# Differential attention in a decoder trunk: weights times values in full fp32 instead of two fp32r halves

## The chip, the core and the metric

The kernel runs as one program on one core of a Trainium2 chip. The metric is the device time of one execution in microseconds; the time quoted for a kernel is the median of its timed runs. One further execution is recorded by the hardware profiler, and all durations of single instructions come from that one.

## The reference

Two layers work on a sequence of 1024 rows of width 1024, everything in float32. Each layer has a token mixer (a convolution group, four heads of differential attention, a gated spatial group, joined by one output projection) and a feed-forward mixer (up-projection, a convolution of width 3, a gate, down-projection). Each ends in a layer norm. The change concerns the attention, which for each head and each block of 128 query rows computes this:

```python
s = jnp.einsum("bhmqd,bhmkd->bhmqk", qb, kb) * scale      # two score maps, m = 0, 1
p = jax.nn.softmax(jnp.where(mask, s, -jnp.inf), axis=-1)
a = p[:, :, 0] - lam * p[:, :, 1]
outs.append(jnp.einsum("bhqk,bhke->bhqe", a, vb))         # vb: 128 values a row
...
o = rms_norm(o, subln_g) * (1.0 - lam_init)
```

## The kernel before

All tensors sit on 128 partitions. Most matrix products are made in the reduced format fp32r: each operand is split into a high part, `hi`, and the rest, `lo`, and three products (hi by hi, hi by lo, lo by hi) are added up in PSUM (`mm3`, L128). A split is a copy by ScalarE and a subtraction by VectorE or GpSimd (`split`, L123).

A layer runs through these stages. `stage1` (L632) makes the projections: first the convolution group's, then the values (`stage_v`, L486), the spatial group (`stage_c`) and queries and keys of four heads (`qk_head`), which go to DRAM. The 62 taps of the depthwise convolution (`conv_taps`, L404) are VectorE work that is handed out in small portions beside these products (`pump`, L93). Then comes the attention (`attention`, L832): four heads, each with eight query blocks of 128 rows, called units here. Unit i reads i+1 key tiles of 128 rows, so a head has 36 key tiles and the two layers together have 288. `stage3` (L909) drives the units, and beside them come the loads of the residual, the splitting of the output projection's weights and the products of the groups that are ready (`out_fill`, L870; tiles `of`). After the attention follow the rest of the output projection (`out_group`, tiles `og`), the norm and the feed-forward mixer.

A unit (`attn_unit`, L742) runs through these steps. TensorE makes two score maps in PSUM (L738, L740). VectorE takes their row maxima (L759, L761). ScalarE makes the exponentials and their row sums (L764). VectorE takes the reciprocals of the sums (L767), a factor `rho` of one number per row (L769), and the difference of the two maps, in place in `p` (L772). TensorE transposes that difference, tile by tile, into PSUM (L783). ScalarE copies it out as the high part (L786) and VectorE makes the low part (L787). TensorE multiplies both with the values (L791, L792). The values `vp` hold a high and a low part side by side, so each product has 256 columns, and the result in PSUM has two halves that still have to be added. ScalarE scales one half (L794), VectorE adds the scaled other half (L795), and ScalarE squares the sum for the norm of the head (L797).

The values get their two parts in `stage_v`: VectorE adds the bias (L492), ScalarE copies the high part (L496), VectorE subtracts (L497), and both go to DRAM in `d_v`.

The order of instructions on each engine is set by a list scheduler at build time, which follows the order of the code, priorities and its own estimates; the up-projection alone has its order written by hand. Buffers come from pools by name: `raw` has 3 buffers, `tmp`, `Ra` and `Rb` have 4 each. `pump` and the late modulation steps are held back until a marked instruction has been issued; for the late steps of layer 0 that mark is `unit_end`, the instruction at L795.

Of the kernel before, what the change touches and what calls it, by code (L numbers as in the profile page):

```python
# [12 lines left out]
F32 = mybir.dt.float32  # L13
F32R = mybir.dt.float32r
BF16 = mybir.dt.bfloat16
I32 = mybir.dt.int32
AF = mybir.ActivationFunctionType
ALU = mybir.AluOpType
AX = mybir.AxisListType

P = 128
D = 1024
S = 1024
L = 2
# [26 lines left out]
class Trunk:  # L51
# [104 lines left out]
    def setup(self):  # L156
        nc, a = self.nc, self.a
        self.ident = self.cst("ident", [P, P])
        make_identity(nc, self.ident)
        self.identb = self.cst("identb", [P, P], BF16)  # L160
        nc.vector.tensor_copy(self.identb, self.ident)
        self.maskb = self.cst("maskb", [P, P], BF16)
        nc.gpsimd.memset(self.maskb, 0.0)
        nc.gpsimd.affine_select(out=self.maskb, in_=self.maskb, pattern=[[-1, P]], compare_op=ALU.is_ge, fill=NEG,
                                base=0, channel_multiplier=1)
        self.ones = self.cst("ones", [P, 1])
        nc.vector.memset(self.ones, 1.0)
        self.mhalf = self.cst("mhalf", [P, 16])
        nc.vector.memset(self.mhalf, -0.5)
        self.cact = self.cst("cact", [P, KT])  # L170
        craw = self.sm("craw", [P, KT], bufs=1)
        nc.sync.dma_start(craw, a["c_t"])
        nc.scalar.activation(out=self.cact, in_=craw, func=AF.Silu)
        self.pc = []
        for l in range(L):
            t = self.cst(f"pc{l}", [P, NPC])
            nc.sync.dma_start(t, a["pcol"][l])
            self.pc.append(t)
        self.rope_c = self.cst("rope_c", [P, 2])
        nc.sync.dma_start(self.rope_c, a["rope_c"])  # L180
        self.lam_cols()
        d = lambda nm, sh, dt=F32: self.dram.tile(list(sh), dt, name=nm, tag=nm, bufs=1)
        self.d_trig = d("d_trig", [2, P, S])
        self.d_q = [d(f"d_q{l}", [4, P, 2, S]) for l in range(L)]
        self.d_k = [d(f"d_k{l}", [4, P, 2, S]) for l in range(L)]
        self.d_v = [d(f"d_v{l}", [4, P, NT, 256]) for l in range(L)]
        self.d_yb = [d(f"d_yb{l}", [2, P, S]) for l in range(L)]
        self.d_xb = d("d_xb", [NT, P, D])
        self.d_act = [d(f"d_act{l}", [NF, P, S]) for l in range(L)]
        self.d_r = [d(f"d_r{l}", [NT, P, D]) for l in range(L)]  # L190
        self.d_gab = d("d_gab", [L, 2, 2 * KT, P])
# [294 lines left out]
    def stage_v(self, l, H, O):  # L486
        nc = self.nc
        brow = self.bias_row(l, 0, 512)

        def evac(tp, ps):  # L490
            vf = self.page("tmp", "vf", shape=(P, 2, 4, P))
            nc.vector.tensor_tensor(out=vf.rearrange("p t h e -> p t (h e)"), in0=ps.rearrange("p (t e) -> p t e", t=2),  # L492
                                    in1=brow.unsqueeze(1).to_broadcast([P, 2, 512]), op=ALU.add)
            for tt in range(2):
                vh = self.page("Ra", "vhl", F32R, (P, 4, 2, P))
                nc.scalar.copy(vh[:, :, 0, :], vf[:, tt])  # L496
                nc.vector.tensor_tensor(out=vh[:, :, 1, :], in0=vf[:, tt], in1=vh[:, :, 0, :].bitcast(F32),  # L497
                                        op=ALU.subtract)
                nc.sync.dma_start(self.d_v[l][:, :, tp * 2 + tt, :].rearrange("h p e -> p h e"),
                                  vh.bitcast(F32).rearrange("p h x e -> p h (x e)"))  # L500
            self.pump(14)
        self.proj_tm(l, 0, H, O, evac)

# [128 lines left out]
    def stage1(self, l, H, O, pre):  # L632
# [31 lines left out]
        for _ in gn:  # L664
            pass
        self.lhs_a(O)
        vp = [self.load_vp(l, 0, i) for i in range(2)]
        self.lhsB, self.lhs0, self.wB = [], [], []
        self.at = O + "c"
        att = self.attention(l, self.X, O, stk, vp, grow)  # L670
# [49 lines left out]
        nc.sync.dma_start(k.bitcast(F32), self.d_k[l][h])  # L720
        return [q[:, 0], q[:, 1], k[:, 0], k[:, 1]]

    def load_vp(self, l, h, i):
        v = self.page("raw", "vp", F32R, (P, 4, 256))
        self.nc.sync.dma_start(v.bitcast(F32), self.d_v[l][h, :, i * 4:(i + 1) * 4, :])
        return v

    def score(self, ps, stk, i):
# [13 lines left out]
    def attn_unit(self, l, at, stk, vp, i, ot, ss):  # L742
# [20 lines left out]
        for m in range(2):  # L763
# [2 lines left out]
        rc = self.sm("rc", [P, 2], bufs=4)  # L766
        nc.vector.reciprocal(out=rc, in_=sums)  # L767
        rho = self.sm("rho", [P, 1], bufs=4)
        nc.vector.scalar_tensor_tensor(out=rho, in0=sums[:, 0:1], scalar=self.nlam[l], in1=rc[:, 1:2],  # L769
                                       op0=ALU.mult, op1=ALU.mult)  # L770
        ad = pr[0]
        nc.vector.scalar_tensor_tensor(out=ad[:, :w], in0=pr[1][:, :w], scalar=rho, in1=ad[:, :w],  # L772
                                       op0=ALU.mult, op1=ALU.add)
        if small:
            a2 = self.page(at, "at", F32R)
            ah, al = a2[:, 0:512], a2[:, 512:1024]
        else:
            ah, al = self.page(at, "ath", F32R), self.page(at, "atl", F32R)
        for b0 in range(0, i + 1, 4):
            b1 = min(i + 1, b0 + 4)  # L780
            pb = self.bank("at")
            for j in range(b0, b1):
                nc.tensor.transpose(pb[:, (j - b0) * P:(j - b0 + 1) * P], ad[:, j * P:(j + 1) * P], self.ident)  # L783
            n = (b1 - b0) * P
            bs = slice(b0 * P, b1 * P)
            nc.scalar.copy(ah[:, bs], pb[:, :n])  # L786
            nc.vector.tensor_tensor(out=al[:, bs], in0=pb[:, :n], in1=ah[:, bs].bitcast(F32), op=ALU.subtract)  # L787
        po = self.bank("pv")
        for j in range(i + 1):
            js = slice(j * P, (j + 1) * P)  # L790
            nc.tensor.matmul(po[:, 0:256], ah[:, js], vp[j // 4][:, j % 4, :], start=j == 0, stop=False)  # L791
            nc.tensor.matmul(po[:, 0:256], al[:, js], vp[j // 4][:, j % 4, :], start=False, stop=j == i)  # L792
        o = ot[:, i, :]
        nc.scalar.activation(out=o, in_=po[:, 128:256], func=AF.Identity, scale=rc[:, 0:1])  # L794
        self.unit_end = nc.vector.scalar_tensor_tensor(out=o, in0=po[:, 0:128], scalar=rc[:, 0:1], in1=o, op0=ALU.mult,  # L795
                                                       op1=ALU.add)
        nc.scalar.activation(out=po[:, 256:384], in_=o, func=AF.Square, accum_out=ss[:, i:i + 1])  # L797

    def head_end(self, l, h, O, ot, ss, halves=(0, 1)):
# [32 lines left out]
    def attention(self, l, H, O, stk, vp, grow):  # L832
        pend = None
        for h in range(4):
            ot = self.page("rows", "ot", shape=(P, NT, P))
            ss = self.sm("oss", [P, NT])
            for n, i in enumerate((7, 6, 3, 5, 2, 4, 1, 0) if h < 3 else (7, 6, 5, 4, 0, 1, 2, 3)):
# [10 lines left out]
                        next(late, None)  # L848
                if n == (1 if h else 4) and h + 1 < 4:
                    nxt = self.load_stacks(l, h + 1, H)  # L850
                    nvp = [self.load_vp(l, h + 1, 0)]
                k = {(2, 3): 0, (2, 5): 1, (2, 7): 2, (3, 0): 3}.get((h, n))
                if k is not None:
                    if k < 2:
                        self.lhs0.append(self.load_yb(l, k, O))
                    self.wB.append(self.load_wout(l, 2 + k, O, grow, self.page(O + "a", "wout")))
                if n == 6 and h + 1 < 4:
                    nvp.append(self.load_vp(l, h + 1, 1))
                if h == 3 and n == 4:
                    self.head_end(l, h, O, ot, ss, (1,))  # L860
                yield
# [571 lines left out]
```

## Time and profile before

| what | value |
|---|---|
| median of 3 runs | 2542.33 us (2537.85 to 2546.43) |
| profiled execution: time, span of its instructions | 2538.86 us, 2537.2 us |
| TensorE busy in the span | 2354.1 us (93%) |
| VectorE busy | 2066.2 us (81%) |
| ScalarE busy | 1066.0 us (42%) |
| GpSimd busy | 395.1 us (16%) |
| mean granted TensorE clock | 0.959 |
| attention stages, by the tiles that TensorE writes | about 290 to 530 us and 1548 to 1795 us |

PE is TensorE's matrix product, PEld its weight load, DVE is VectorE, ACT is ScalarE, POOL is GpSimd, SP issues the DMAs. The recorded end of a product is modelled and products overlap, so TensorE's pace is read from the distance between starts. PEclk is the share of its full clock that TensorE was granted. In a table by stretches, "x96" is the number of instructions that began in the stretch.

### The profile page before, as it was taken

To read this page: it belongs to the slowest core of one execution; us is meant where nothing else is said; L and a number is where in the kernel's file an instruction comes from. 1 tells how busy PE (TensorE), PEld (TensorE's weight loads), DVE (VectorE), ACT (ScalarE), POOL (GpSimd) and SP (SyncE) were. 2 spreads that over 40 slices of the span, in tenths; PEclk is the share of its full clock that TensorE was granted. 3 is DMA by queue.
4 is the path that set the end of the run, shared out by engine and by line. 5 is a ranking of instruction groups with operands and counts; after the bars stand their busy time and mean duration, and the time that the engine had idled before them with its cause. 6 is when DMAs were issued, how large, how long until landed. Compare 5 with 4: busy or idle time off the path is not lost. (4 is left out here: it accounts for less than half of the span.)

```text
span 2537.2 us, 28532 instructions
## 1 busy us (share of the span) xinstructions
PE 2354.1 (93%) x10846; PEld 1912.6 (75%) x10846; DVE 2066.2 (81%) x2794; ACT 1066.0 (42%) x1708; POOL 395.1 (16%) x213
## 2 busy tenths in 40 slices
PE   8999989988999999999789999999899999989996
PEld 7777768766888887788578776777678888868885
DVE  7998787889887888778979987768887777797768
ACT  4314744645554554311131157445554554552111
POOL 1243160433000000000020542213510000000003
PEclk9998979999999999999889998999899999999998
DMA  8443433222332334645513244220322222254311
GB/s 295 152 153 130 160 142 117 75 100 71 112 110 90 117 108 155 206 142 182 172 61 133 87 160 164 95 108 32 108 75 83 84 83 83 84 183 148 100 42 67
DMA packets 88826, 302.47 MB, mean 119 GB/s; under 512 B 9392, under 2 KB 18928, under 8 KB 87152
## 3 DMA queue, kind: packets, MB, share of 16 engines
q1 hardware_dynamic: 88688, 300.65, 34.9%
q8 instruction: 85, 1.39, 0.2%
q14 instruction: 53, 0.43, 0.1%
HBM read 232.42 MB, written 68.19 MB: 118 GB/s over the span
## 5 line engine op out<-in xcount | busy, mean ns | idle before, releaser
L130 PE MATMUL og<-dn,dn 128*128 128x512 f32 x704 | 281.2, 399 | 37.6 <-DVE r L905 21.6
L1092 PE MATMUL upb<-comb,uw 128*128 128x512 f32 x704 | 275.9, 392 | 10.9 <-DVE upc L1116 6.7
L131 PE MATMUL og<-dn,dn 128*128 128x512 f32 x704 | 278.5, 396 | 0.0
L132 PE MATMUL og<-dn,dn 128*128 128x512 f32 x704 | 278.3, 395 | 0.0
L1093 PE MATMUL upb<-comb,uw 128*128 128x512 f32 x704 | 275.4, 391 | 2.7 <-DVE comb L980 2.7
L1094 PE MATMUL upb<-comb,uw 128*128 128x512 f32 x704 | 274.9, 391 | 0.0
L1116 DVE TENSOR_TENSOR uw<-wu,uw 128x512 fp32r<-128x512 f32 x210 | 144.2, 687 | 125.3 <-ACT uw L1119 125.3
L138 POOL TENSOR_TENSOR lnrs<-lnrs,mhalf 128x1 f32<-128x1 f32 x32 | 20.8, 653 | 1386.1 <-DVE lnrs L137 1374.4
L905 DVE TENSOR_TENSOR r<-og,r 128x1024 f32<-128x1024 f32 x144 | 174.6, 1219 | 66.8 <-PE og L132 66.0
L1129 DVE SCALAR_TENSOR_TENSOR cv<-upc,pc,cv 128x1023 f32<-128x1023 f32 (+1 forms) x176 | 225.4, 1281 | 2.8
L130 PEld LDWEIGHTS og<-dn,dn 128*128 128x128 f32 x704 | 134.5, 191 | 72.1 <-DVE r L905 27.2
L410 DVE SCALAR_TENSOR_TENSOR convacc<-convy,pc,convacc 128x1023 f32<-128x1023 f32 (+14 forms) x120 | 178.7, 1489 | 1.8
L125 ACT CAST dn<-actr 128x1024 fp32r<-128x1024 f32 x44 | 46.0, 1049 | 306.5 <-PE og L131 146.2
L1092 PEld LDWEIGHTS upb<-comb,uw 128*128 128x128 f32 x704 | 132.7, 188 | 41.6 <-DVE upc L1116 8.4
L1119 ACT CAST uw<-wu 128x512 fp32r<-128x512 f32 x210 | 121.7, 616 | 83.6 <-DVE wu L1116 77.1
L1093 PEld LDWEIGHTS upb<-comb,uw 128*128 128x128 f32 x704 | 132.8, 189 | 31.8 <-DVE comb L980 4.5
L132 PEld LDWEIGHTS og<-dn,dn 128*128 128x128 f32 x704 | 134.4, 191 | 28.2
L131 PEld LDWEIGHTS og<-dn,dn 128*128 128x128 f32 x704 | 134.8, 192 | 27.4
L1094 PEld LDWEIGHTS upb<-comb,uw 128*128 128x128 f32 x704 | 132.7, 189 | 27.6
L1093 PE MATMUL upd<-comb,uw 128*128 128x512 f32 x352 | 138.1, 392 | 5.9 <-DVE comb L980 5.9
L1092 PE MATMUL upd<-comb,uw 128*128 128x512 f32 x352 | 137.7, 391 | 0.0
L1094 PE MATMUL upd<-comb,uw 128*128 128x512 f32 x352 | 137.3, 390 | 0.0
(327 smaller groups left out, 5812.1 us busy)
## 6 DMA issues: line engine op xcount, KB each, us to landing
wada<-in_w_ada SPq DMA_DIRECT2D x96, 512.0 KB, 4.5
wu<-in_w_up_t SPq DMA_DIRECT2D x84, 512.0 KB, 3.6
d_act<-cv SPq DMA_DIRECT2D x44, 512.0 KB, 2.6
actr<-d_act SPq DMA_DIRECT2D x44, 512.0 KB, 4.2
wdn<-in_w_down SPq DMA_DIRECT2D x44, 512.0 KB, 4.2
win<-in_w_fm SPq DMA_DIRECT2D x24, 512.0 KB, 4.5
wtm<-in_w_tm SPq DMA_DIRECT2D x16, 512.0 KB, 3.7
d_v<-vhl SPq DMA_DIRECT2D x16, 512.0 KB, 2.9
```

Of the source, the lines that this page charges most:

```text
L125: nc.scalar.copy(hi, src)
L130: mm(ps, lh, rh, start=first, stop=False)
L131: mm(ps, lh, rl, start=False, stop=False)
L132: mm(ps, ll, rh, start=False, stop=last)
L410: nc.vector.scalar_tensor_tensor(out=acc[:, d:], in0=y[:, :S - d], scalar=w(30 - d), in1=acc[:, d:], op0=ALU.mult, op1=ALU.add)
L905: nc.vector.tensor_tensor(out=r[t], in0=ps, in1=r[t], op=ALU.add)
L1092: mm(ps, w[:, 0, ks], hi[k], start=k == 0 and not more, stop=False, skip_group_check=True)
L1093: mm(ps, w[:, 0, ks], lo[k], start=False, stop=False, skip_group_check=True)
L1094: mm(ps, w[:, 1, ks], hi[k], start=False, stop=k == 3, skip_group_check=True)
L1116: v.tensor_tensor(out=o, in0=x, in1=y, op=op)
L1119: act.copy(self.up_w[n][:, 0], src)
L1129: v.scalar_tensor_tensor(out=u[:, d:], in0=c[:, :S - d], scalar=self.ffw[:, 2 - d, m:m + 1], in1=u[:, d:], op0=ALU.mult, op1=ALU.add)
```

## The change

The weights are no longer split. ScalarE copies the transposed difference out of PSUM as plain float32, one product per key tile multiplies it with plain float32 values of 128 columns, and the result needs no addition: one ScalarE operation scales it on its way out of PSUM. The values are stored once, without a low part: `d_v` has half its size, a head's values fit into one buffer of `raw` instead of two and come with one load, and the buffer after the bias comes from `Ra` instead of `tmp`. The factor `rho` is made by a tensor_scalar with two scalars per row from one tensor, instead of a scalar_tensor_tensor with two tensors. A unit takes one buffer for the transposed weights (a large unit took two). The mark `unit_end` moves to the difference (L772 of before).

```diff
-        self.d_v = [d(f"d_v{l}", [4, P, NT, 256]) for l in range(L)]
+        self.d_v = [d(f"d_v{l}", [4, P, NT, P]) for l in range(L)]
...
         def evac(tp, ps):
-            vf = self.page("tmp", "vf", shape=(P, 2, 4, P))
+            vf = self.page("Ra", "vf", shape=(P, 2, 4, P))
             nc.vector.tensor_tensor(out=vf.rearrange("p t h e -> p t (h e)"), in0=ps.rearrange("p (t e) -> p t e", t=2),
                                     in1=brow.unsqueeze(1).to_broadcast([P, 2, 512]), op=ALU.add)
             for tt in range(2):
-                vh = self.page("Ra", "vhl", F32R, (P, 4, 2, P))
-                nc.scalar.copy(vh[:, :, 0, :], vf[:, tt])
-                nc.vector.tensor_tensor(out=vh[:, :, 1, :], in0=vf[:, tt], in1=vh[:, :, 0, :].bitcast(F32),
-                                        op=ALU.subtract)
-                nc.sync.dma_start(self.d_v[l][:, :, tp * 2 + tt, :].rearrange("h p e -> p h e"),
-                                  vh.bitcast(F32).rearrange("p h x e -> p h (x e)"))
+                nc.sync.dma_start(self.d_v[l][:, :, tp * 2 + tt, :].rearrange("h p e -> p h e"), vf[:, tt])
...
-    def load_vp(self, l, h, i):
-        v = self.page("raw", "vp", F32R, (P, 4, 256))
-        self.nc.sync.dma_start(v.bitcast(F32), self.d_v[l][h, :, i * 4:(i + 1) * 4, :])
+    def load_vp(self, l, h):
+        v = self.page("raw", "vp", shape=(P, NT, P))
+        self.nc.sync.dma_start(v, self.d_v[l][h])
         return v
...
-        nc.vector.scalar_tensor_tensor(out=rho, in0=sums[:, 0:1], scalar=self.nlam[l], in1=rc[:, 1:2],
-                                       op0=ALU.mult, op1=ALU.mult)
+        nc.vector.tensor_scalar(out=rho, in0=rc[:, 1:2], scalar1=sums[:, 0:1], scalar2=self.nlam[l], op0=ALU.mult,
+                                op1=ALU.mult)
         ad = pr[0]
-        nc.vector.scalar_tensor_tensor(out=ad[:, :w], in0=pr[1][:, :w], scalar=rho, in1=ad[:, :w],
+        self.unit_end = nc.vector.scalar_tensor_tensor(out=ad[:, :w], in0=pr[1][:, :w], scalar=rho, in1=ad[:, :w],
                                        op0=ALU.mult, op1=ALU.add)
-        if small:
-            a2 = self.page(at, "at", F32R)
-            ah, al = a2[:, 0:512], a2[:, 512:1024]
-        else:
-            ah, al = self.page(at, "ath", F32R), self.page(at, "atl", F32R)
+        a = self.page(at, "at")
...
-            nc.scalar.copy(ah[:, bs], pb[:, :n])
-            nc.vector.tensor_tensor(out=al[:, bs], in0=pb[:, :n], in1=ah[:, bs].bitcast(F32), op=ALU.subtract)
+            nc.scalar.copy(a[:, b0 * P:b1 * P], pb[:, :(b1 - b0) * P])
         po = self.bank("pv")
         for j in range(i + 1):
-            js = slice(j * P, (j + 1) * P)
-            nc.tensor.matmul(po[:, 0:256], ah[:, js], vp[j // 4][:, j % 4, :], start=j == 0, stop=False)
-            nc.tensor.matmul(po[:, 0:256], al[:, js], vp[j // 4][:, j % 4, :], start=False, stop=j == i)
+            nc.tensor.matmul(po[:, 0:P], a[:, j * P:(j + 1) * P], vp[:, j, :], start=j == 0, stop=j == i)
         o = ot[:, i, :]
-        nc.scalar.activation(out=o, in_=po[:, 128:256], func=AF.Identity, scale=rc[:, 0:1])
-        self.unit_end = nc.vector.scalar_tensor_tensor(out=o, in0=po[:, 0:128], scalar=rc[:, 0:1], in1=o, op0=ALU.mult,
-                                                       op1=ALU.add)
+        nc.scalar.activation(out=o, in_=po[:, 0:P], func=AF.Identity, scale=rc[:, 0:1])
```

The scheduler orders the instructions anew. VectorE of before, in layer 0, from the middle of the first head's units (`rc`, `rho`, `p`, `mx` and `at` are the tiles of the unit's steps above, `z` is the key projection of head 3):

```order
L767 RECIPROCAL rc_2400<-sums_2376 128x2
L759 TENSOR_REDUCE mx_2485<-sc_2486 128x1
L769 SCALAR_TENSOR_TENSOR rho_2402<-sums_2376,nlam_103,rc_2400 128x1
L767 RECIPROCAL rc_2456<-sums_2441 128x2
L772 SCALAR_TENSOR_TENSOR p_2380<-p_2381,rho_2402,p_2380 128x896
L769 SCALAR_TENSOR_TENSOR rho_2458<-sums_2441,nlam_103,rc_2456 128x1
L529 TENSOR_TENSOR z_2279<-z_2279,rot_2278 128x1024
L759 TENSOR_REDUCE mx_2485<-sc_2487 128x1
L772 SCALAR_TENSOR_TENSOR p_2444<-p_2444,rho_2458 128x512
L795 SCALAR_TENSOR_TENSOR ot_2211<-pv_2258,rc_2237,ot_2211 128x128
L761 TENSOR_REDUCE mx_2547<-sc_2548 128x2
L787 TENSOR_TENSOR atl_2406<-at_2407,ath_2405 128x512
```

The same units on VectorE of the changed kernel (its lines 754, 756, 762, 764 and 767 are L759, L761, L767, L769 and L772 of before, its 524 is L529):

```order
L762 RECIPROCAL rc_2362<-sums_2338 128x2
L764 TENSOR_SCALAR rho_2364<-rc_2362,sums_2338,nlam_103 128x1
L754 TENSOR_REDUCE mx_2430<-sc_2431 128x1
L767 SCALAR_TENSOR_TENSOR p_2342<-p_2343,rho_2364,p_2342 128x896
L762 RECIPROCAL rc_2407<-sums_2392 128x2
L524 TENSOR_TENSOR z_2241<-z_2241,rot_2240 128x1024
L754 TENSOR_REDUCE mx_2430<-sc_2432 128x1
L764 TENSOR_SCALAR rho_2409<-rc_2407,sums_2392,nlam_103 128x1
L756 TENSOR_REDUCE mx_2482<-sc_2483 128x2
L767 SCALAR_TENSOR_TENSOR p_2395<-p_2395,rho_2409 128x512
```

Between the difference of one unit and the maxima of the next there is no subtraction and no addition any more, and `rho` follows its reciprocal.

TensorE of before, at the first unit's product with the values (`pv`), beside the fill (`of`) and the next score map (`sc`):

```order
L130 MATMUL of_4053<-woh_2358,yah_2130 128x512
L791 MATMUL pv_2258<-vp_2138,ath_2242 128x256
L738 MATMUL sc_2486<-stk_1934,stk_1930 128x512
L738 MATMUL sc_2486<-stk_1934,stk_1932 128x512
L738 MATMUL sc_2486<-stk_1936,stk_1930 128x512
```

And in the changed kernel:

```order
L130 MATMUL of_3781<-woh_2320,yah_2106 128x512
L778 MATMUL pv_2229<-vp_2114,at_2216 128x128 x8
L131 MATMUL of_3781<-wol_2321,yah_2106 128x512
L132 MATMUL of_3781<-woh_2320,yal_2107 128x512
L733 MATMUL sc_2431<-stk_1910,stk_1906 128x512
L733 MATMUL sc_2431<-stk_1910,stk_1908 128x512
```

The eight products of the unit stand in one piece ahead of the next score map. Before, one product with the high part stood ahead of that map, and the other fifteen, low and high in turn, came in pieces behind it.

More of the change, by code (lines that the diff above doesn't have):

```diff
@@ L666, in stage1 @@
         self.lhs_a(O)
-        vp = [self.load_vp(l, 0, i) for i in range(2)]
+        vp = self.load_vp(l, 0)
         self.lhsB, self.lhs0, self.wB = [], [], []
@@ L783, in attn_unit @@
                 nc.tensor.transpose(pb[:, (j - b0) * P:(j - b0 + 1) * P], ad[:, j * P:(j + 1) * P], self.ident)
-            n = (b1 - b0) * P
-            bs = slice(b0 * P, b1 * P)
-            nc.scalar.copy(ah[:, bs], pb[:, :n])
-            nc.vector.tensor_tensor(out=al[:, bs], in0=pb[:, :n], in1=ah[:, bs].bitcast(F32), op=ALU.subtract)
+            nc.scalar.copy(a[:, b0 * P:b1 * P], pb[:, :(b1 - b0) * P])
         po = self.bank("pv")
         for j in range(i + 1):
-            js = slice(j * P, (j + 1) * P)
-            nc.tensor.matmul(po[:, 0:256], ah[:, js], vp[j // 4][:, j % 4, :], start=j == 0, stop=False)
-            nc.tensor.matmul(po[:, 0:256], al[:, js], vp[j // 4][:, j % 4, :], start=False, stop=j == i)
+            nc.tensor.matmul(po[:, 0:P], a[:, j * P:(j + 1) * P], vp[:, j, :], start=j == 0, stop=j == i)
         o = ot[:, i, :]
-        nc.scalar.activation(out=o, in_=po[:, 128:256], func=AF.Identity, scale=rc[:, 0:1])
-        self.unit_end = nc.vector.scalar_tensor_tensor(out=o, in0=po[:, 0:128], scalar=rc[:, 0:1], in1=o, op0=ALU.mult,
-                                                       op1=ALU.add)
+        nc.scalar.activation(out=o, in_=po[:, 0:P], func=AF.Identity, scale=rc[:, 0:1])
         nc.scalar.activation(out=po[:, 256:384], in_=o, func=AF.Square, accum_out=ss[:, i:i + 1])
@@ L850, in attention @@
                     nxt = self.load_stacks(l, h + 1, H)
-                    nvp = [self.load_vp(l, h + 1, 0)]
+                    nvp = self.load_vp(l, h + 1)
                 k = {(2, 3): 0, (2, 5): 1, (2, 7): 2, (3, 0): 3}.get((h, n))
@@ L856, in attention @@
                     self.wB.append(self.load_wout(l, 2 + k, O, grow, self.page(O + "a", "wout")))
-                if n == 6 and h + 1 < 4:
-                    nvp.append(self.load_vp(l, h + 1, 1))
                 if h == 3 and n == 4:
```

## The prediction

> **What bounds the kernel now.** I looked first at the whole span: TensorE is busy almost everywhere, so a gain must come from places where it is not. A table by slices shows these places in the two attention stages, most of all where GpSimd is at work. So I cut the attention into stretches. First those in which GpSimd is busy; the columns are start and end, length, busy time (and instructions) of PE, PEld, DVE, ACT and POOL, PEclk, DMA share, GB/s; the last line is their sum.
>
> ```profile
> 318.00:346.00 28.00, 21.51 (x96) 17.67 (x97) 28.00 (x28) 12.16 (x28) 24.99 (x9) 0.66 0.37 141
> 450.00:480.00 30.00, 27.10 (x142) 20.47 (x141) 26.46 (x41) 19.88 (x51) 21.97 (x9) 0.83 0.37 123
> 1578.00:1598.00 20.00, 14.52 (x69) 11.78 (x70) 19.96 (x21) 11.14 (x23) 16.38 (x6) 0.79 0.55 213
> 1700.00:1730.00 30.00, 25.57 (x120) 19.57 (x121) 24.86 (x37) 19.26 (x52) 20.22 (x9) 0.72 0.25 89
> sum 108.00, PE 88.70 PEld 69.49 DVE 99.29 ACT 62.44 POOL 83.56; mean PE 22.18 PEld 17.37 DVE 24.82 ACT 15.61 POOL 20.89
> ```
>
> VectorE is busy for 99.29 of these 108 us (92%), TensorE starts 428 instructions in them, and its clock falls to 0.66 to 0.83. The rest of the two stages, five of its seven stretches and the sum of all seven:
>
> ```profile
> 290.00:318.00 28.00, 22.80 (x86) 16.21 (x84) 15.91 (x16) 22.45 (x30) 4.74 (x2) 0.82 0.45 172
> 370.00:450.00 80.00, 79.50 (x478) 65.14 (x477) 59.23 (x107) 34.52 (x103) 3.29 (x2) 1.00 0.31 108
> 480.00:530.00 50.00, 43.36 (x255) 33.77 (x255) 38.14 (x78) 22.66 (x71) 12.17 (x8) 1.00 0.07 22
> 1548.00:1578.00 30.00, 25.83 (x98) 18.00 (x96) 16.86 (x15) 25.27 (x33) 4.79 (x2) 0.83 0.42 156
> 1598.00:1700.00 102.00, 99.72 (x575) 80.05 (x573) 67.10 (x127) 44.45 (x129) 3.76 (x3) 0.99 0.24 88
> sum 379.00, PE 352.12 PEld 276.62 DVE 266.86 ACT 190.50 POOL 53.87; mean PE 50.30 PEld 39.52 DVE 38.12 ACT 27.21 POOL 7.70
> ```
>
> Here the fill keeps TensorE at work: 478 instructions in 80 us against 96 in 28, with VectorE at about 70%. So VectorE is the bound in the first set, TensorE in most of the second.
>
> Why VectorE is full in the first set, the chronology of GpSimd (two lines) and of VectorE (six) shows:
>
> ```profile
> 324.46 5.53 POOL L126 TENSOR_TENSOR wol<-wout,woh 128x1024 fp32r<-128x1024 f32 x2
> 329.95 8.49 POOL L889 TENSOR_TENSOR r<-r,ab 128x1024 f32<-128x1024 f32 x3
> ...
> 324.45 0.15 DVE L767 RECIPROCAL rc<-sums 128x2 f32<-128x2 f32 x1
> 324.57 3.21 DVE L772 SCALAR_TENSOR_TENSOR p<-p,rho,p 128x896 f32<-128x896 f32 x1
> 327.70 2.31 DVE L769 SCALAR_TENSOR_TENSOR rho<-sums,nlam,rc 128x1 f32<-128x1 f32 x1
> 333.82 0.34 DVE L795 SCALAR_TENSOR_TENSOR ot<-pv,rc,ot 128x128 f32<-128x128 f32 x1
> ...
> 346.88 0.22 DVE L769 SCALAR_TENSOR_TENSOR rho<-sums,nlam,rc 128x1 f32<-128x1 f32 x1
> 347.13 0.88 DVE L772 SCALAR_TENSOR_TENSOR p<-p,rho,p 128x640 f32<-128x640 f32 x1
> ```
>
> One number per row costs `rho` 2.31 us while GpSimd works and 0.22 us when it does not, and the difference (L772) grows to 3.21 us. Both read two tensors from SBUF. L795, with one input from PSUM, and the reciprocal, with one input, keep their 0.34 and 0.15 us. So each `rho` and each difference waits for about one instruction of GpSimd (5.53 us for two).
>
> **The change part by part.** Each pair of lines is the busy time of one line of the code on VectorE, first in the 108 us, then in the 379 us: L787 (low part of the weights), L795 (the addition), L769 (`rho`), L772 (the difference). The last line is L137, an operation of one number per row with one tensor from SBUF, which stands all over the program: how many there are, and the shortest, median and longest in ns.
>
> ```profile
> sum 108.00, DVE 12.06; mean DVE 3.01
> sum 379.00, DVE 40.23; mean DVE 5.75
> ...
> sum 108.00, DVE 3.88; mean DVE 0.97
> sum 379.00, DVE 18.24; mean DVE 2.61
> ...
> sum 108.00, DVE 21.84; mean DVE 5.46
> sum 379.00, DVE 12.11; mean DVE 1.73
> ...
> sum 108.00, DVE 32.91; mean DVE 8.23
> sum 379.00, DVE 39.98; mean DVE 5.71
> ...
> L137 DVE TENSOR_SCALAR lnrs<-lnmv x32: 134/140/155, 540.1 to 2526.2; 128x1 f32<-128x1 f32 x32
> ```
>
> *In the 108 us.* L787 and L795 go: 12.06 + 3.88 = 15.9 us. `rho` becomes an operation with one tensor; L137 never took over 0.155 us, so I price it at 0.15, or 9.6 us for all 64 units. A third of these, 3.2 us, I put here, more than the stretches' share of the time (108 of 487 us), and 18.6 us go. Together 34.5 us. Since VectorE is the bound for 92% of the time, 32 us of it come off the path. TensorE is late next: at the pace of the filled stretch (478 in 80 us) its 428 instructions need 72 us, so no more than 36 could come off; 32 stands.
>
> *In the 379 us.* 40.23 + 18.24 us go, and of `rho` 12.11 less the other 6.4 us: 64 us of VectorE. But TensorE leaves only 379 − 352 = 27 us here, and 9 of these lie in the two opening stretches, where the key projection of head 3 and ScalarE set the pace. Of the other 18 I take half off the path, 8 us: some waits for the low part, for the addition, and for the buffers that both hold.
>
> *The values' stage.* These are its two stretches in which TensorE falls behind, and the subtraction that goes:
>
> ```profile
> 140.00:220.00 80.00, 70.16 (x309) 57.40 (x307) 79.53 (x88) 12.76 (x14) 31.22 (x16) 0.96 0.33 112
> 1430.00:1480.00 50.00, 45.63 (x194) 37.03 (x192) 47.46 (x59) 9.48 (x11) 27.56 (x14) 0.97 0.03 11
> L497 DVE TENSOR_TENSOR vhl<-vf,vhl 128x512 fp32r<-128x512 f32 x16 | 17.9, 1122 | 0.0
> ```
>
> VectorE works off the taps without a pause, and 17.9 us of it go. TensorE is idle for 9.8 + 4.4 = 14.2 us there; two thirds of that, 9 us, come off. ScalarE's sixteen copies and half of the bytes to DRAM go too; neither engine nor queue is late there, so I count nothing.
>
> *The product with the values.* What it costs in full fp32 the trace does not show, since its full-fp32 products have one column. The chronology of TensorE, three places (a start, a duration, an instruction in each line):
>
> ```profile
> 381.15 0.39 PE L131 MATMUL of<-wol,ych 128*128 128x512 f32 x1
> 381.38 0.39 PE L132 MATMUL of<-woh,ycl 128*128 128x512 f32 x1
> 381.60 0.28 PE L792 MATMUL pv<-vp,atl 128*128 128x256 f32 x1
> 381.71 0.28 PE L791 MATMUL pv<-vp,ath 128*128 128x256 f32 x1
> 381.83 0.28 PE L792 MATMUL pv<-vp,atl 128*128 128x256 f32 x1
> ...
> 435.91 1.40 PE L269 MATMUL modp<-ones,wada 128*128 128x1 f32 x12
> 437.17 0.63 PE L783 MATMUL at<-ident,p 128*128 128x128 f32 x4
> ```
>
> The pair for one key tile now takes 0.23 us from start to start, as long as one product of 512 columns in fp32r (0.23). The full-fp32 product of one column takes (437.17 − 435.91) / 12 = 0.105 us, nearly all of it the load of its weights. That is the low end for the new product: 288 × (0.105 − 0.23) = −36 us on TensorE. The high end is four such loads one behind the other with 128 columns (0.23 / 4) behind each: 4 × 0.163 = 0.65 us, +121 us. Between them I take 0.23, the row of the pair that it replaces, for the same operands and the same multiplications: no change. The Trainium skill, on the page FP8 and Floating Point Precision, section TensorE Precision Notes, says that true FP32 makes four passes through the array. An estimate from that is four times 128 columns, as long as the row of 512, 0.23 us, and the sum would stay as it is. No run here shows it yet.
>
> *At no cost:* one load of a head's values instead of two (a buffer of `raw` comes free, and nothing new waits), and the earlier mark for layer 0's late steps: they are VectorE work and find the room of the removed 64 us; without that room each would delay a maximum.
>
> The sum: 32 + 8 + 9 = 49 us off the profiled execution's 2538.86 us, so 2490. The median of the three runs lies 3.5 us higher, and they spread over 0.34%, which is why a difference within 0.3% counts as none.
>
> **The rivals.**
> *More comes off.* Without the wait of `rho`, GpSimd's instruction may no longer slip in between it and the difference. L772 at its price of the other stretches (39.98 us for two thirds of the units) would take 20 us instead of 32.91 for the third, 13 us less; and TensorE's idle 18 us could go in full, 10 more. Then 2467. Against it: 83.56 us of GpSimd stay in those stretches.
>
> *The wait only moves.* `rho` no longer waits, but the difference then arrives earlier in GpSimd's instruction and waits longer. Then 17 of the 32 us are not gained: 2507. For it speaks that L772 reads two tensors as before. The Trainium skill, on the page SBUF — State Buffer, section Who interferes with whom, says that a VectorE instruction with two SBUF inputs contends with a GpSimd instruction that reads SBUF and one with a single input, outside the two-port modes, does not. The rows of L772, L769 and L795 agree; whether two scalars per row count as inputs none of them shows.
>
> *Another chain takes over.* The score maps hold PSUM until the maxima and exponentials are done, and this loop keeps its length:
>
> ```profile
> ACT p L764 <- DVE mx L759: 45.3, 26, 5.5
> ```
>
> If that loop is next, half of the 32 us come off, and none of the 8: 2538.86 − 16 − 9 = 2514. Against it: the maxima are themselves queued behind the operations that go.
>
> *Slower:* the full-fp32 product loads its weights anew for each pass and waits for it, 0.65 us. Of the 121 us, the share of the filled stretches (379 of 487 us) is paid in full, 94 us, and 49 come off: 2584. It decides from where 288 × 0.78 × extra reaches 49 us, at 0.22 us extra, 0.45 us a product. For it speaks that weights dominate the one-column row; against it, that the weight loads of fp32r products (busy 276.62 of 379 us) do not lengthen their spacing of 0.23.
>
> **How the numbers follow.** Forecast 0.46; more comes off 0.17; the wait moves 0.12; another chain 0.13; the costly product 0.12, of which two parts in twelve fall short of the point that makes it slower. Within 0.3% (2531 to 2546) come these two and 4 of the chain's 13, which could leave even less; so faster 0.84, same 0.06, slower 0.10. The range goes from 2450 (more comes off, and the cheap end of the product adds to it) to 2535 (the chain's case, with a product a little dearer than the pair); it leaves out the costly product and a little at either end.
>
> **What would show it.** Right: `rho` at about 0.15 us throughout; VectorE less busy by about 110 us; both attention stages shorter by 15 to 25 us each and the taps done earlier; `pv` starts 0.23 us apart; the clock in the four stretches nearer 1. Wrong: `pv` starts over 0.45 us apart; `rho` of over 2 us still; L772 at over 3 us more often than now; attention stages as long as before with TensorE waiting for exponentials.

## The result, and the profile after

The changed kernel takes 2483.64 us (median of 4 runs, 2482.01 to 2485.9) against 2541.22 us of the kernel before on the same chip (4 runs, 2537.85 to 2546.43): a ratio of 0.9772, 95% interval 0.9753 to 0.9792. That is 57.6 us faster. The forecast was 2490, the range 2450 to 2535. The profiled execution took 2485.14 us.

The head of the page of the changed kernel:

```profile
span 2483.4 us, 28299 instructions
PE 2323.6 (94%) x10846; PEld 1889.5 (76%) x10846; DVE 1988.7 (80%) x2618; ACT 1049.6 (42%) x1692; POOL 402.4 (16%) x213
```

VectorE lost 77.5 us of work (2066.2 before) and TensorE 30.5 (2354.1 before).

Where the time came from is read by cutting both spans at the same events: the first or last product into a tile that marks a stage. Attention here runs from the last product of the projection before it (`prf`) to the last product of the fill (`of`).

| stage, us | before | after | difference |
|---|---|---|---|
| start to attention, layer 0 | 312.0 | 311.9 | −0.1 |
| attention, layer 0 | 219.8 | 195.6 | −24.2 |
| rest of layer 0, and on to the first product of the values (`ptm`) in layer 1 | 820.8 | 817.9 | −2.9 |
| projections of layer 1 from there (to its attention) | 220.1 | 215.2 | −4.9 |
| attention, layer 1 | 212.2 | 191.2 | −21.0 |
| rest | 752.3 | 751.6 | −0.7 |

Of the 53.8 us between the two spans 45 lie in the two attention stages. A table by stretches of these two stages, changed kernel (columns as in the prediction's tables: start and end, length, busy time and instructions of PE, PEld, DVE, ACT, POOL, then PEclk, DMA share, GB/s):

```profile
312.00:507.00 195.00, 184.78 (x1098) 146.12 (x1097) 139.74 (x204) 104.75 (x291) 73.81 (x32) 0.98 0.32 113
1541.00:1732.00 191.00, 183.04 (x1083) 144.16 (x1084) 125.34 (x194) 104.65 (x292) 53.22 (x24) 0.99 0.25 90
sum 386.00, PE 367.83 PEld 290.28 DVE 265.08 ACT 209.39 POOL 127.02; mean PE 183.91 PEld 145.14 DVE 132.54 ACT 104.70 POOL 63.51
```

And the kernel before:

```profile
312.00:532.00 220.00, 200.51 (x1101) 158.33 (x1100) 173.79 (x284) 107.59 (x293) 74.10 (x33) 0.91 0.31 109
1573.00:1785.00 212.00, 194.49 (x1080) 153.70 (x1079) 159.22 (x273) 107.26 (x290) 53.04 (x25) 0.94 0.25 92
sum 432.00, PE 395.00 PEld 312.03 DVE 333.00 ACT 214.85 POOL 127.14; mean PE 197.50 PEld 156.02 DVE 166.50 ACT 107.42 POOL 63.57
```

Read the sums as a balance. The stages are 46 us shorter with as many TensorE instructions, 2181. TensorE's idle time fell from 432 − 395.00 = 37.0 to 386 − 367.83 = 18.2 us, which is 18.8 us. The other 27.2 us are busy time: as many instructions took less of it, and the granted clock rose from 0.91 and 0.94 to 0.98 and 0.99. Scaling by the clock alone gives 200.51 × 0.91/0.98 + 194.49 × 0.94/0.99 = 370.9 us, where 367.83 were measured; so by this estimate the clock accounts for about 24 of the 27.2 us. In these stages, then, waits that go were gained about twice: as the waits themselves, and as clock for what TensorE does around them. The Trainium skill, on the page TensorE: Matmul & The Clock Gate, section What's actually happening, says that the clock follows how busy the array was of late; these sums agree, but a stretch of the 64-column kernel below does not follow from the busy time alone. That the clock follows the waits is read from the tables and from runs that bring waits back; the clock itself was not set in any run.

The stretches of the changed kernel in which GpSimd works hardest, which answer to the four of the prediction:

```profile
318.00:338.00 20.00, 18.61 (x106) 14.44 (x104) 18.78 (x24) 14.19 (x35) 18.89 (x7) 0.83 0.57 214
440.00:482.00 42.00, 39.16 (x256) 30.83 (x255) 35.33 (x54) 31.20 (x89) 27.02 (x11) 1.00 0.23 69
1541.00:1558.00 17.00, 15.23 (x96) 11.51 (x97) 15.11 (x18) 14.32 (x30) 10.50 (x4) 1.00 0.71 280
1656.00:1704.00 48.00, 47.67 (x311) 37.23 (x310) 41.38 (x65) 35.13 (x97) 27.11 (x11) 1.00 0.27 88
```

In three of them the clock is full and TensorE starts about 6 instructions per us; before it started 3.4 to 4.7. In the first, with a clock of 0.83, VectorE is still busy for 18.78 of 20 us.

Two of VectorE's operations that stand beside GpSimd, the difference (two groups) and `rho` (busy us in total, mean ns of one, then idle time before them), kernel before:

```profile
L772 DVE SCALAR_TENSOR_TENSOR p<-p,rho,p 128x1024 f32<-128x1024 f32 (+3 forms) x32 | 42.9, 1341 | 0.6
L772 DVE SCALAR_TENSOR_TENSOR p<-p,rho 128x512 f32<-128x512 f32 (+3 forms) x32 | 30.0, 937 | 0.7
L769 DVE SCALAR_TENSOR_TENSOR rho<-sums,nlam,rc 128x1 f32<-128x1 f32 x64 | 33.9, 530 | 1.3
```

Changed kernel:

```profile
L767 DVE SCALAR_TENSOR_TENSOR p<-p,rho,p 128x1024 f32<-128x1024 f32 (+3 forms) x32 | 46.0, 1438 | 1.0
L767 DVE SCALAR_TENSOR_TENSOR p<-p,rho 128x512 f32<-128x512 f32 (+3 forms) x32 | 25.3, 790 | 0.7
L764 DVE TENSOR_SCALAR rho<-rc,sums,nlam 128x1 f32<-128x1 f32 x64 | 17.3, 271 | 1.8
```

`rho` went from 33.9 to 17.3 us, while the difference has all but kept its time: 71.3 us, against 72.9 before.

### The profile page after: what moved, and what is told of

It is laid out like the page before. It is cut to its first block, busy times and chain, and to the rows that moved or that the text cites. A ratio compares the mean times of both kernels' runs of the same rounds, so it can differ in the third digit from the quotient of the medians.

```text
span 2483.4 us, 28299 instructions
## 1 busy us (share of the span) xinstructions
PE 2323.6 (94%) x10846; PEld 1889.5 (76%) x10846; DVE 1988.7 (80%) x2618; ACT 1049.6 (42%) x1692; POOL 402.4 (16%) x213
## 4 chain that ended last, share of the span: by engine, by line
PE 37%; DVE 9%; issue 3%; ACT 3%; POOL 2%; DMA 1%; SPq 0%; POOLq 0%; DVEq 0%; ACTq 0%
PE og L130 3%; PE og L131 3%; PE og L132 3%; PE upb L1074 3%; PE upb L1076 3%; PE upb L1075 3%; PE sc L733 2%; PE upd L1076 1%; PE upd L1074 1%; PE upd L1075 1%; PE pv L778 1%; DVE r L887 1%; PE of L130 1%; DVE dn L126 1%; PE of L132 1%
```

## The experiments

Ratios are against the kernel before on the same chip; 0.001 is 2.5 us. "Against the changed kernel" is the distance to its 0.9772, whose own interval is 0.0039 (10 us) wide. Every edit also makes the scheduler order the instructions anew, so a single run holds more than its edit. The last two columns are the lengths of attention in the profiled execution, read as in the table above.

| kernel | ratio, 95% interval | against the changed kernel | attention 0 | attention 1 |
|---|---|---|---|---|
| changed kernel | 0.9772 [0.9753, 0.9792] | | 195.6 | 191.2 |
| `rho` as before | 0.9852 [0.9838, 0.9865] | +20 us | 210.0 | 202.7 |
| low part of the weights back | 0.9819 [0.9806, 0.9833] | +12 us | 203.0 | 201.5 |
| values' split back | 0.9820 [0.9807, 0.9834] | +12 us | 204.8 | 190.3 |
| addition back | 0.9828 [0.9813, 0.9844] | +14 us | 207.5 | 197.4 |
| all four back | 0.9964 [0.9952, 0.9976] | +49 us | 217.3 | 211.6 |
| each product twice | 1.0028 [1.0018, 1.0039] | +65 us | 222.8 | 229.6 |
| 64 columns | 0.9847 [0.9827, 0.9867] | +19 us | 216.4 | 191.9 |
| 256 columns | 0.9955 [0.9937, 0.9972] | +46 us | 222.1 | 215.2 |
| low parts of the output projection's operands on VectorE | 0.9789 [0.9773, 0.9804] | +4 us | 200.5 | 194.4 |
| kernel before with the new `rho` alone | 0.9911 [0.9893, 0.9928] | | 208.8 | 205.3 |

**`rho` as before, in the changed kernel.**

```diff
-        nc.vector.tensor_scalar(out=rho, in0=rc[:, 1:2], scalar1=sums[:, 0:1], scalar2=self.nlam[l], op0=ALU.mult,
-                                op1=ALU.mult)
+        nc.vector.scalar_tensor_tensor(out=rho, in0=sums[:, 0:1], scalar=self.nlam[l], in1=rc[:, 1:2],
+                                       op0=ALU.mult, op1=ALU.mult)
```

> The changed kernel with rho made again by the old operation with two tensors. Theory (the waits of rho for GpSimd were on the path): rho again costs about 34 us of VectorE in all instead of 17, and the time rises by 10 to 17 us, to 2494 to 2501. Rival (the wait only moves to the difference of the maps): rho is dearer but the difference cheaper by as much, and the time rises by 0 to 4 us, to at most 2488.

It costs 20 us, more than either theory gave. VectorE's order here is nearly that of the changed kernel, so the two chronologies can be laid side by side. With the old `rho`, from one step of the key projection to the third unit's difference:

```profile
317.56 1.22 DVE L522 TENSOR_TENSOR z<-z,rot 128x1024 f32<-128x1024 f32 x1
...
318.89 2.15 DVE L764 SCALAR_TENSOR_TENSOR rho<-sums,nlam,rc 128x1 f32<-128x1 f32 x1
320.96 0.95 DVE L754 TENSOR_REDUCE mx<-sc 128x1 f32<-128x768 f32 x1
321.83 2.45 DVE L767 SCALAR_TENSOR_TENSOR p<-p,rho,p 128x896 f32<-128x896 f32 x1
...
328.37 1.44 DVE L764 SCALAR_TENSOR_TENSOR rho<-sums,nlam,rc 128x1 f32<-128x1 f32 x1
...
330.61 2.06 DVE L767 SCALAR_TENSOR_TENSOR p<-p,rho 128x512 f32<-128x512 f32 x1
...
332.78 2.14 DVE L764 SCALAR_TENSOR_TENSOR rho<-sums,nlam,rc 128x1 f32<-128x1 f32 x1
334.96 3.08 DVE L767 SCALAR_TENSOR_TENSOR p<-p,rho,p 128x768 f32<-128x768 f32 x1
```

The same steps in the changed kernel:

```profile
318.13 1.21 DVE L522 TENSOR_TENSOR z<-z,rot 128x1024 f32<-128x1024 f32 x1
...
319.45 0.27 DVE L764 TENSOR_SCALAR rho<-rc,sums,nlam 128x1 f32<-128x1 f32 x1
320.43 0.96 DVE L754 TENSOR_REDUCE mx<-sc 128x1 f32<-128x768 f32 x1 [0.71 <-PE sc L735]
321.31 1.23 DVE L767 SCALAR_TENSOR_TENSOR p<-p,rho,p 128x896 f32<-128x896 f32 x1
...
326.63 0.26 DVE L764 TENSOR_SCALAR rho<-rc,sums,nlam 128x1 f32<-128x1 f32 x1
...
327.68 0.92 DVE L767 SCALAR_TENSOR_TENSOR p<-p,rho 128x512 f32<-128x512 f32 x1
...
328.71 0.27 DVE L764 TENSOR_SCALAR rho<-rc,sums,nlam 128x1 f32<-128x1 f32 x1
329.02 2.62 DVE L767 SCALAR_TENSOR_TENSOR p<-p,rho,p 128x768 f32<-128x768 f32 x1
```

From `z` to the third difference it takes 17.4 us with the old `rho` (317.56 to 334.96) and 10.9 with the new (318.13 to 329.02): 6.5 us over three units. The three `rho` give 4.9 of these (5.73 against 0.80 us). The differences wait longer too, 7.59 against 4.77 us for the three; part of that VectorE spends idle in the changed kernel (0.71 us ahead of a maximum). So the difference doesn't wait in `rho`'s place: with the old `rho` both wait. Over both attention stages:

```profile
311.00:521.00 210.00, 189.47 (x1101) 150.27 (x1100) 150.46 (x204) 105.11 (x292) 69.65 (x32) 0.95 0.30 107
1557.00:1759.00 202.00, 190.53 (x1081) 150.00 (x1082) 128.19 (x194) 105.03 (x292) 49.72 (x24) 0.94 0.24 88
sum 412.00, PE 379.99 PEld 300.26 DVE 278.64 ACT 210.14 POOL 119.37; mean PE 190.00 PEld 150.13 DVE 139.32 ACT 105.07 POOL 59.69
```

VectorE has 13.6 us more work than in the changed kernel (278.64 against 265.08). TensorE's idle time rises by 13.8 us (32.0 against 18.2) and its busy time by 12.2, at a clock of 0.95 and 0.94. The loss is again made of waits and clock, in about equal parts, which is how 13.6 us of VectorE can cost more than themselves: 26 us in the stages of this execution, the longest of its five.

**The new `rho` alone, in the kernel before** (the same two lines, the other way round).

> The kernel before with only rho changed to the operation with two scalars. Theory (its waits for GpSimd are on the path): minus 10 to 17 us, 2524 to 2531. Rival (the wait only moves to the difference): 0 to minus 4 us, 2537 to 2541, and the difference grows by what rho loses.

It is worth about 23 us there (0.0089 of 2541), beyond what was expected again: 11.0 us come off the first attention stage and 6.9 off the second. The rival would have had the difference grow by what `rho` loses; `rho` lost 16.7 us (33.9 to 17.2) and the difference grew by 3.1 (72.9 to 76.0). So `rho` is the largest of the four parts that were put back one by one, and it is worth as much in the kernel before; the other three were not tried from that side.

**The low part of the weights back, read by nobody.**

```diff
+        al = a[:, 512:1024] if small else self.page(at, "atl")
...
             nc.scalar.copy(a[:, b0 * P:b1 * P], pb[:, :(b1 - b0) * P])
+            nc.vector.tensor_tensor(out=al[:, b0 * P:b1 * P], in0=pb[:, :(b1 - b0) * P],
+                                    in1=a[:, b0 * P:b1 * P], op=ALU.subtract)
```

> The changed kernel with the subtraction of the low part put back on VectorE, into buffers of its own, but with nobody reading it: the product does not wait for it. Theory (VectorE's load was the bound where GpSimd works, and a third of its 52 us on the path): plus 15 to 25 us, 2499 to 2509. Rival (what came off is the wait of the product for the low part): plus 0 to 5 us, at most 2489.

It costs 12 us, a little short of the theory and well over the rival. Its groups:

```profile
L767 DVE SCALAR_TENSOR_TENSOR p<-p,rho,p 128x1024 f32<-128x1024 f32 (+3 forms) x32 | 52.2, 1631 | 0.6
L777 DVE TENSOR_TENSOR atl<-at,at 128x512 f32<-128x512 f32 x64 | 35.4, 581 | 6.5 <-ACT at L776 6.2
L767 DVE SCALAR_TENSOR_TENSOR p<-p,rho 128x512 f32<-128x512 f32 (+3 forms) x32 | 35.3, 1102 | 0.5
```

Besides 35.4 us of subtraction the difference grew from 71.3 to 87.5 us; why was not followed up. About 52 us of VectorE cost 12 us of time, so most of it lies beside TensorE's work.

**The addition back.** VectorE goes over the scaled result once more, adding PSUM times zero.

```diff
         nc.scalar.activation(out=o, in_=po[:, 0:P], func=AF.Identity, scale=rc[:, 0:1])
+        nc.vector.scalar_tensor_tensor(out=o, in0=po[:, 0:P], scalar=0.0, in1=o, op0=ALU.mult, op1=ALU.add)
```

> The changed kernel with one thing back: after ScalarE has scaled a unit's result, VectorE runs over the same 128x128 once more (PSUM result times 0.0 plus the scaled result), as long as the removed addition was, between the scaling and the square. The result stays the same. Theory (each VectorE operation that a unit gives up shortens the attention, by about half of its time, as the low part did: 14 us for 37 us): 22 us of VectorE come back, so plus 6 to 12 us, 0.980 of the time before. Rival (the addition stood behind the products, where nothing of the next unit waits for it): plus 0 to 3 us, 0.977 to 0.9785.

It costs 14 us, a little over the theory; the rival is out. Its group:

```profile
L781 DVE SCALAR_TENSOR_TENSOR ot<-pv,ot 128x128 f32<-128x128 f32 x64 | 18.3, 286 | 18.3 <-ACT ot L780 18.1
```

The figure behind the second bar matters: VectorE also stood idle for 18.3 us ahead of these additions until ScalarE had scaled the result (L780). Its queue is in order, so what stands behind the addition waits with it, which doubles the 18.3 us of work. Before, L795 had such a wait too (13.9 us), and the prediction counted only the work.

**The values' split back** (a copy, a subtraction and the buffer from `tmp`; its low part is not read).

```diff
-            vf = self.page("Ra", "vf", shape=(P, 2, 4, P))
+            vf = self.page("tmp", "vf", shape=(P, 2, 4, P))
...
+                vh = self.page("Ra", "vhl", shape=(P, 4, 2, P))
+                nc.scalar.copy(vh[:, :, 0, :], vf[:, tt])
+                nc.vector.tensor_tensor(out=vh[:, :, 1, :], in0=vf[:, tt], in1=vh[:, :, 0, :], op=ALU.subtract)
```

> The changed kernel with the copy and the subtraction of the values' low part put back in the values' stage; nobody reads their result. Theory from the two traces (only layer 1 gained there): plus 3 to 6 us, 2487 to 2490. As the prediction had it (both layers gained): plus 8 to 10 us, 2492 to 2494. Rival (the stage is bound by TensorE and the gain there has another cause): 0 to 2 us.

12 us is more than any of the theories gave, and it doesn't lie where the work was put. In front of layer 0's attention nothing is lost, in front of layer 1's 4.5 us; 9.2 us are lost in layer 0's attention, which the edit doesn't touch, and layer 1's attention is about as long as in the changed kernel (190.3 against 191.2). The loss lies in the first units. Their first 43 us, here and then in the changed kernel:

```profile
312.00:355.00 43.00, 36.99 (x190) 27.92 (x188) 34.80 (x37) 26.09 (x64) 35.33 (x13) 0.79 0.60 232
312.00:355.00 43.00, 41.11 (x237) 31.28 (x236) 38.20 (x44) 29.39 (x74) 35.89 (x13) 0.92 0.65 247
```

TensorE starts 47 instructions fewer, at a clock of 0.79 instead of 0.92. What was bought with the values' work is therefore about 4.5 us. What set off the 9.2 us was not tried by itself; the new order of VectorE's work beside GpSimd's is a guess. A single experiment here can't be trusted to better than about that, and the 64-column kernel below shows still more.

**All four back.** What stays of the change is the product in full fp32, which doesn't wait for the low part, the smaller transfers and the earlier mark.

> The changed kernel with all of VectorE's work back (rho with two tensors, the low part of the weights, the subtraction and copy for the values, the addition), the new parts unread; what stays of the change is the product itself, one in full fp32 of 128 columns instead of two in fp32r of 256, the smaller transfer of the values, and the earlier mark. The result stays the same. Theory (the gain is VectorE's work, the product is neutral): within 0.4% of the time before, 0.995 to 1.002. Rival (the products standing in one piece, or free of the low part, are a gain of their own, and the single parts overlap): 0.984 to 0.992. The opposite (the single losses add up to more than the gain since each run is a new order): over 1.004.

The theory holds: 0.9964 [0.9952, 0.9976], 49 us behind the changed kernel and 6 to 12 us ahead of the one before. The four single losses add up to 59 us; together they are 49, and 42 of these lie in the two attention stages. The attention of this kernel, by the same stretches:

```profile
314.00:531.00 217.00, 196.66 (x1100) 155.16 (x1100) 174.17 (x284) 107.00 (x292) 74.11 (x33) 0.92 0.28 99
1570.00:1782.00 212.00, 191.53 (x1086) 150.57 (x1085) 158.47 (x274) 107.02 (x292) 54.03 (x25) 0.93 0.24 86
```

VectorE's time (174.17 and 158.47 us) and the clock (0.92 and 0.93) are those of the kernel before. Of the 9 us that are left only 3 lie in the attention (428.9 against 432.0 us), where TensorE is busy for 395.00 − 388.19 = 6.8 us less; which of the things left gives them was not separated.

**Each product twice.** The second adds the same again, so the result doubles before it is normalised.

```diff
-            nc.tensor.matmul(po[:, 0:P], a[:, j * P:(j + 1) * P], vp[:, j, :], start=j == 0, stop=j == i)
+            for x in range(2):
+                nc.tensor.matmul(po[:, 0:P], a[:, j * P:(j + 1) * P], vp[:, j, :], start=j + x == 0,
+                                 stop=j == i and x == 1)
```

> The changed kernel with each product of weights and values made twice into the same sum, so that its output is twice as large before the norm of the head. 288 times 0.22 = 64 us more for TensorE. If TensorE is the bound of the attention after the change: plus 45 to 64 us, 2529 to 2548. If other chains are: plus 10 to 30 us, 2494 to 2514.

The group of the products in the changed kernel, and then in this one:

```profile
L778 PE MATMUL pv<-vp,at 128*128 128x128 f32 x576 | 80.4, 283 | 0.4 <-ACT at L775 0.3
```

```profile
L779 PE MATMUL pv<-vp,at 128*128 128x128 f32 x1152 | 146.5, 282 | 0.9 <-ACT at L775 0.8
```

The trace has 576 records for the 288 products: one product in full fp32 is two instructions. The second set costs (146.5 − 80.4) / 288 = 0.23 us a product, and the kernel loses 65 us for these 66 us. The attention stages are 65.6 us longer. What is added to TensorE's work there is paid in full, so with VectorE's work gone TensorE is the bound.

**64 and 256 columns.** The number of columns of the product is changed. With 64, half of the values is left out, and the operation that scales the result writes its 64 columns twice; with 256, the next key tile's values are multiplied too, and the last key tile takes the values of its neighbour.

```diff
-            nc.tensor.matmul(po[:, 0:P], a[:, j * P:(j + 1) * P], vp[:, j, :], start=j == 0, stop=j == i)
+            nc.tensor.matmul(po[:, 0:64], a[:, j * P:(j + 1) * P], vp[:, j, 0:64], start=j == 0, stop=j == i)
...
-            nc.tensor.matmul(po[:, 0:P], a[:, j * P:(j + 1) * P], vp[:, j, :], start=j == 0, stop=j == i)
+            k = min(j, NT - 2)
+            nc.tensor.matmul(po[:, 0:256], a[:, j * P:(j + 1) * P], vp[:, k:k + 2, :].rearrange("p t e -> p (t e)"),
+                             start=j == 0, stop=j == i)
```

> The changed kernel with only the first 64 of the 128 value columns multiplied; the result is written twice, so half of the output of each head is left out. If the load of the weights sets the pace of a full fp32 product: the starts of pv stay 0.11 us apart and the time stays within 3 us of 2484. If the columns set it: 0.06 us apart, 32 us less of TensorE, and 2460 to 2475.

> The changed kernel with each product over 256 value columns, two key tiles of the values side by side, of which the first 128 columns are used; for the last key tile these are the wrong ones. If the load of the weights sets the pace: starts 0.11 to 0.12 us apart and the time within 4 us of 2484. If the columns set it, in two passes for each record: 0.21 us apart, 58 us more of TensorE, and 2510 to 2540.

The same group with 64 columns, and with 256:

```profile
L778 PE MATMUL pv<-vp,at 128*128 128x64 f32 x576 | 81.5, 286 | 0.1
```

```profile
L779 PE MATMUL pv<-vp,at 128*128 128x256 f32 x576 | 141.6, 386 | 0.2
```

Half of the columns save nothing (81.5 against 80.4 us); twice as many cost (141.6 − 80.4) / 576 = 0.106 us for each record. In the trace the records start 0.112 us apart with 64 and with 128 columns and 0.216 apart with 256 (medians inside a unit). So at 64 and at 128 columns something that doesn't depend on the columns sets the pace, which the load of the weights would explain, and at 256 the columns do; the time of that kernel, 2533.57 us, lies in the range that went with the columns. The time of the 64-column kernel fits neither theory: its 19 us lie in layer 0's attention alone, where the clock was 0.89, while layer 1's takes 191.9 us against 191.2. Most of the loss is clock. TensorE is busy there for 201.90 us instead of 184.78 and idle for 15.1 instead of 10.2. The same 20 us, in this kernel and in the changed one:

```profile
330.00:350.00 20.00, 19.60 (x79) 15.36 (x79) 13.38 (x17) 9.32 (x29) 20.00 (x9) 0.50 0.49 184
330.00:350.00 20.00, 20.00 (x110) 16.00 (x110) 18.18 (x25) 12.46 (x40) 20.00 (x9) 0.83 0.56 211
```

TensorE was granted half of its clock though it was busy for 19.60 of the 20 us, and VectorE was not short of time (13.38 of 20). So the clock is not a matter of TensorE's busy share alone. Its instructions stand in another order there; why the clock stayed low was not settled.

**Low parts of the output projection's operands on VectorE.** GpSimd's 24 subtractions for these (the weights, the convolution group and the first heads) move to VectorE; 18 of them lie in the attention stages.

```diff
-            self.split(hi, lo, self.ya[c])
+            self.split(hi, lo, self.ya[c], self.nc.vector)
...
-        self.split(hi, lo, raw)
+        self.split(hi, lo, raw, nc.vector)
...
-        self.split(hi, lo, raw)
+        self.split(hi, lo, raw, self.nc.vector)
```

> The changed kernel with the low parts of the output projection's operands in the attention (weights, convolution group, first heads) made by VectorE instead of GpSimd: 24 operations, 62 us less for GpSimd, about 29 us more for VectorE. Theory (what VectorE loses in the attention are waits for GpSimd's instructions, over 2 us each): minus 3 to 12 us, 2472 to 2481. Rival (VectorE's own load is the bound there): plus 5 to 20 us.

The attention of this kernel:

```profile
sum 396.00, PE 373.49 PEld 294.91 DVE 282.36 ACT 211.81 POOL 80.63; mean PE 186.74 PEld 147.46 DVE 141.18 ACT 105.90 POOL 40.32
```

GpSimd lost 46 us of work there and the difference fell from 71.3 to 63.3 us, but VectorE as a whole rose by 17.3 us, and the time is no shorter: the expected gain (0.9725 to 0.976 as a ratio) lies outside the interval, and 4 us more is just short of the rival's 5 to 20. With this exchange the waits for GpSimd could not be bought off with VectorE's own time.

## Why the prediction was right, and where its steps were off

*The bound.* VectorE's work and its waits for GpSimd in the attention were the cause, as forecast: restoring that work alone, with the new product kept, gives back 49 of the 57.6 us. The attention gained 45 us where the two terms (32 and 8) came to 40. How the 45 divide between GpSimd's stretches and the rest was not measured, since the stretches do not match one to one. Between the two profiled executions 53.7 us came off, where the sum had 49.

*The clock* has no term in the sum, and the measured balance gives it about 24 of the 46 us. Part of it was in the forecast without being named: the limit of 36 us in GpSimd's stretches is the pace of a stretch whose clock was 1.00, and only 108 − 88.70 = 19.3 us of it were idle time of TensorE. (The four counts add up to 427 instructions, not 428, which changes nothing.) In the other stretches the 8 us were taken from idle time alone, so what the clock gained there was put at nothing without a reason. That the sum came out near is partly luck: the attention's 40 us were 5 too low, the values' stage 4 too high.

*`rho`* takes 0.27 us, not 0.15: the row of L137 was an operation with one constant in place of the two scalars per row. All 64 of them cost 17.3 us instead of 9.6. That it never waits for GpSimd, although its two scalars lie in SBUF, was forecast and holds: the mean over all 64 is 271 ns and the longest takes 276, in GpSimd's stretches and outside. The Trainium skill, on the page SBUF — State Buffer, section Who interferes with whom, says that a VectorE instruction with two SBUF inputs contends with a GpSimd instruction that reads SBUF, and that one with at most one SBUF input, outside the two-port modes, does not; scalars per row do not count as such an input in the rows of `rho`. That an operation with one tensor is always spared would be too wide a reading, though. The same line L137 on eight columns takes 2.32 us beside GpSimd in the changed kernel, just ahead of a `rho`:

```profile
461.40 2.32 DVE L137 TENSOR_SCALAR oss<-oss 128x8 f32<-128x8 f32 x1
...
463.82 0.27 DVE L764 TENSOR_SCALAR rho<-rc,sums,nlam 128x1 f32<-128x1 f32 x1
```

The median of these rows of `oss` is 0.172 us. So what is shown for `rho` is shown for an operation on one column.

*VectorE's busy time* fell by 77.5 us, not by about 110 (the prediction's own terms, 34.5 + 64 + 17.9, add up to 116). The removed work is there: L787, L795, L497 and half of `rho` are 52.9 + 22.1 + 17.9 + 16.6 = 109.5 us. But the durations of all VectorE instructions together fell by 94 us, so others took some 15 us longer, 7 of them the rotation of the queries and keys (`z<-z,rot`). The other 17 us are bookkeeping: instructions of VectorE overlap in the trace, and busy time counts an overlap once. The difference kept its waits; that is why the first rival, that its waits shrink, didn't come, nor the second, that they grow.

*The values' stage* was given 9 us. In layer 0 it gained nothing, in layer 1 4.9 us. The stretch of layer 0 that the prediction used, changed kernel:

```profile
140.00:220.00 80.00, 70.16 (x321) 57.80 (x319) 78.26 (x91) 13.95 (x15) 34.26 (x16) 0.96 0.29 93
```

TensorE is busy for 70.16 us, as before to the digit, though it starts 321 instructions instead of 309. The spatial group's first product across rows (`sv`) then starts 4.6 us earlier (209.5 against 214.1), and the transposes of the finished taps (`gnp`) 2.1 us earlier; by the end of the projections that is given back: their last products start at the same time. Changed kernel, then before:

```profile
L131 PE MATMUL prf<-h,wh x16: 389/393/628, 288.6 to 311.7; 128*128 128x512 f32 x16
```

```profile
L131 PE MATMUL prf<-h,wh x16: 389/394/632, 289.8 to 311.8; 128*128 128x512 f32 x16
```

*The product* was priced at the 0.23 us of the pair that it replaces, and costs 0.23. The Trainium skill, on the page FP8 and Floating Point Precision, section TensorE Precision Notes, has true FP32 make four passes. An estimate from that is that 128 columns take as long as 512 of one pass, and 256 columns twice that; both agree (0.23, and 2 × 0.216 us). That 64 columns take as long as 128 does not follow from it. The low end was read wrongly. The 0.105 us of a one-column product was the distance between two records, and a product is two of them, so its true price was 0.21: no row of the trace allowed a gain of 36 us.

*The slower rival* put its turning point at 0.45 us a product, with the added time paid to 78%. The doubled product costs 0.46 and comes out 0.28% slower than the kernel before, so the point came out right, but by two errors that cancel: the added time is paid in full, and the gain to be used up was larger.

*Another chain* was not seen: TensorE is busy for 95% of both stages.

## What to carry to other kernels

When a stage is short of one engine, look past the busy time that an edit removes: an instruction that waits at the head of an in-order queue costs its wait too (18 us of wait for 18 us of addition), and where idle time on TensorE fell here, by 18.8 us, the clock rose as well, so that a removed wait can pay twice. Look at the granted clock before you blame an engine: one run lost 19 us mostly to a low clock. Give operations on one column that stand between GpSimd's instructions one tensor and scalars rather than two tensors: here one line of that kind was worth about 20 us. Count the records that one product leaves in the trace before you take a price from their distance.

## What the runs showed of the hardware that was not expected

A product in full fp32 stands in the trace as two instructions, 0.112 us apart at 64 and 128 columns and 0.216 at 256, so that 64 columns instead of 128 save nothing.

A tensor_scalar on one number per row with two scalars from SBUF takes 0.27 us, longer than the scalar_tensor_tensor that it replaces does undisturbed (0.22), and yet wins since it does not wait for GpSimd (the old one took up to 2.38 us). A tensor_scalar with one tensor of eight columns did wait (2.32 us).

TensorE's clock can stay at half while TensorE is busy: 0.50 over 20 us in which it was busy for 19.60.

The same work in another order can cost 10 to 20 us: two edits that touch other work (the values' split, 64 columns) moved layer 0's attention by 9 and 21 us and left layer 1's within 1 us.
